# Experts' weights split as pairs of rows, the one-hot table as one VectorE operation, and a buffer of its own for the weighted result

## The chip, the core and the metric

The kernel runs on one core of one Trainium2 chip. The metric is the device time of one execution in microseconds (us); the median of three runs of the kernel before is 1759.38 us. The engines are called PE (TensorE, with PEld for its loads of the stationary operand), DVE (VectorE), ACT (ScalarE), POOL (GpSimd) and SP (SyncE, which here only issues DMA transfers).

## The reference

One layer of a hybrid diffusion model: 1024 latent tokens and 256 context tokens of width 1024 go through differential attention and a gated delta rule, and then the latent tokens through a mixture of 16 experts. Only this last part is touched by the change:

```python
def expert_choice_ffn(h, w_router, w_gate, w_up, w_down):
    def route_set(t):
        n = t.shape[0]
        cap = CAP_FACTOR * n // N_EXPERTS                      # 128 tokens for each expert
        aff = jax.nn.softmax((t @ w_router).astype(jnp.float32), axis=-1)
        gate, idx = lax.top_k(aff.T, cap)                      # each expert chooses its tokens
        xe = t[idx]                                            # 16 x 128 x 1024
        hid = jax.nn.silu(jnp.einsum('ecd,edf->ecf', xe, w_gate)) * jnp.einsum('ecd,edf->ecf', xe, w_up)
        ye = jnp.einsum('ecf,efd->ecd', hid, w_down) * gate[..., None].astype(t.dtype)
        return jnp.zeros_like(t).at[idx.reshape(-1)].add(ye.reshape(-1, t.shape[-1]))
...
x_new = x + gt1 * (jnp.concatenate([o_da, o_gdn], axis=-1) @ w_out)
x_new = x_new + gt2 * expert_choice_ffn(modulate(x_new, norm2_g, sh2, sc2), w_router, w_gate, w_up, w_down)
return rms_norm(x, final_g)
```

Each expert has three float32 matrices of 1024 x 1024 (4 MB each), so that 192 MB of weights are read once, for 128 tokens per expert.

## The kernel before, in words

Products of float32 are made in three passes of a rounded format: each operand is split into a rounded part (`hi`) and its rest (`lo`), and `mm3` (L167) adds hi x hi, lo x hi and hi x lo in PSUM. For one weight row of 1024 values per partition ("a row" below, 128 partitions x 1024) that is 6 matmuls of 128x512, since 1024 columns fill two PSUM banks.

The expert stage (`_experts`) takes, for each expert e, 12 loads of 1 MB, four for each of `w_gate`, `w_up` and `w_down`. `weights` (L1448) issues the load on SP into a buffer `raw` of a ring (`_Ring`; 9 + MORE + 1 buffers in turn) and splits its two rows one after the other: ACT copies the rounded part (`whi`, L1460), DVE subtracts it from the raw row (`wlo`, L1461; for the first few loads POOL does). `whi` and `wlo` have 5 buffers each (WHI, WLO). A raw buffer is free for the next load when its last `wlo` is done; a `whi` or `wlo` buffer is free when PE has used it.

PE's work for an expert is `up` (8 rows of gate into `pgu`, 8 rows of up into `pgv`, in turns of two) and, an expert later, `down` (8 rows of down into `py`): 144 matmuls and 16 transposes. After `up`, ACT takes silu of `pgu` into `hid` (L1505) and DVE multiplies it with `pgv` (L1506); `turned` (L1472) transposes `hid` on PE into the PSUM tile `ptm` and splits it into `hTh` (ACT) and `hTl` (DVE). In the same way the gathered tokens `xe` become `xTh` and `xTl`. `pgu` and `pgv` have one buffer each, so that the next expert's first matmul into `pgu` waits until ACT has read it for `hid`. After `down`, `scatter` weights `py` into `y` on DVE (L1525) and POOL adds its rows to the result in DRAM by an indirect DMA. The tile `y` shares its one buffer with `hid` (tag "hid", YT).

`lists` (L1406) makes an expert's list of tokens two experts ahead: a one-hot table of 128 x 8 x 128, eight `tensor_scalar` operations of 128x128 on DVE for the first four experts and on POOL for the others; eight small matmuls into `pls`, three tiny DVE operations (`ls`, `idx`, `gate`), and then POOL can gather the tokens.

Each engine works through its own queue in order. The order in the queues comes from the scheduler of the tile framework, which places the instructions ahead of time by its own estimates; the kernel's text gives dependencies and priorities only. What stands where is read below from the orders of the two programs.

Of the kernel before, what the change touches and what calls it, by code (L numbers as in the profile page):

```python
"""Hybrid diffusion layer: differential attention and a gated delta rule side by side, then an
expert-choice mixture of experts, on one core.

float32 products of width 256 and more run as three float32r passes over operands that are split
exactly into a rounded part and its rest (h*h + l*h + h*l); narrower ones run in float32.
"""
# [22 lines left out]
P = 128  # L29
# [40 lines left out]
MORE = 6  # L70
WAIT = (16, 17, 18)
YT, RT = "hid", "xe"
WHI, WLO = 5, 5
# [3 lines left out]
# the tokens that the scans finish first come first  # L77
# [31 lines left out]
class _K:  # L109
# [7 lines left out]
    def after(self, dst, src):  # L117
        """A load to dst waits until src is there."""
        self.nc.gpsimd.tensor_copy(dst, src)

    def slot(self, kind, i=None, name=None, dt=F32):
        """A buffer of the queries' or keys' size; in turn, those first that the last head's projections leave first."""
        if i is None:
            order = (0, 1) if kind == "KL" else (0, 2, 1)
            i = order[self.turn[kind] % len(order)]
            self.turn[kind] += 1
        return self.qk.tile([P, L if kind == "QS" else LT], dt, name=name or kind, tag=f"{kind}{i}")
# [4 lines left out]
    def xT(self, kt, t, n):  # L132
        """The two parts of x^T for tiles t to t + n of a group."""
        t0 = max(g for g in self.XT if g <= t)
        return [x[:, kt, (t - t0) * P:(t - t0 + n) * P] for x in self.XT[t0]]
# [9 lines left out]
    def rsqrt_steps(self, pool, x, n, np_=P, tag=""):  # L145
        """1/sqrt(x) for positive x [np_, n]: three Newton steps from the bit estimate."""
# [22 lines left out]
    def mm3(self, out, ah, al, bh, bl, start, stop):  # L169
        """out (+)= a.T @ b in float32, from the split operands."""  # L170
# [10 lines left out]
def _decays(K, pg, ps):  # L181
    """Decays and betas of the delta rule: [token, direction, chunk, head]."""
# [55 lines left out]
def _prep(K, pg, ps, h, kvq):  # L238
    """Norms and decays of a head's chunks, their matrices and the inverses of the 16 x 16 diagonal blocks.

    With k = r k~ (k~ before its l2 norm), c = beta r^2, N = (k~ k~^T) * decay, a chunk of 128 tokens is
        u' = (I + N c)^-1 (v / r - e^G k~ S),   S' = e^Gl S + k~^T (c e^(Gl-G) u'),
        o  = r_q (e^G q~ S + ((q~ k~^T) * decay) c u').
    Both directions share a matrix: below the diagonal the forward one, above it the backward one.
    """
# [29 lines left out]
    # queries with the decay from their chunk's start, one set per direction  # L275
# [59 lines left out]
    # a 16 x 16 block per partition, by substitution  # L335
# [11 lines left out]
    def both(t, fwd, bwd, rows, cols):  # L347
        """A part of both directions' blocks, from an element of each on."""
# [3 lines left out]
    for j in range(15):  # L352
        # forward: rows after j gain their multiple of row j; backward: rows before 15 - j
# [16 lines left out]
def _inproj(K, banks):  # L370
    """Modulation, x^T and the input projection."""
# [7 lines left out]
    with tc.tile_pool(name="p1v", bufs=1, reuse_waits="tile") as pv, \  # L379
# [21 lines left out]
        # v of the attention and a, b of the delta rule, tokens on partitions  # L401
# [15 lines left out]
    # the rest, channels on partitions  # L417
# [109 lines left out]
def _modulation(K, pe, ps, psm):  # L527
    """Shift and scale of both token sets, channels on partitions; loads the first tokens on the way."""
# [23 lines left out]
    # silu(c), silu(c_ctx)  # L552
# [10 lines left out]
    for kt in range(KT):  # L563
# [4 lines left out]
        # of the last tile the scales in float32 at once, the shifts from split parts  # L568
# [26 lines left out]
def _tokens(K, pe, ps, xts, late):  # L595
    """x^T, modulated and split."""
# [31 lines left out]
def _row_vectors(K, pool, ps):  # L628
    """Gate 1, shift 2, scale 2 and gate 2 as rows in DRAM."""
# [29 lines left out]
def _mix(K, prep, left):  # L659
    """Differential attention and the delta rule's scans, side by side."""  # L660
# [3 lines left out]
    with tc.tile_pool(name="g", bufs=1, side="right", reuse_waits="tile") as pg, \  # L664
# [29 lines left out]
        # the first tokens of the output projection, in the buffers that the attention leaves  # L694
# [13 lines left out]
def _mixed(K, t, ol, oh, lo):  # L708
    """The parts of a tile's transposed mix."""
# [12 lines left out]
def _weights(K, pw):  # L722
    """The parts of most of w_out, in the buffers that the last head's scan leaves."""
# [14 lines left out]
    # what the attention's last head leaves  # L738
# [8 lines left out]
    # what is left of them takes the parts of the last head's mix  # L747
# [4 lines left out]
def _weight(K, k, hi, lo, raw):  # L752
    """The parts of a tile of w_out, its columns scaled by the gate."""
# [10 lines left out]
def _delta(K, pg, pw, gps, ps):  # L764
    """Inverses from the 16 x 16 blocks up, T <- T - T (off-diagonal block) T, and the scans of both directions."""
# [27 lines left out]
    def levels(h, st, c0, n):  # L793
        """Doubles the blocks up to the chunk, then W and U of both directions."""
# [50 lines left out]
    def all_levels(h, st):  # L845
        """The chunks' groups in interleaved streams."""
# [4 lines left out]
    # the context's chunks come first  # L851
# [14 lines left out]
    def scan(h, st, step):  # L866
        """One chunk of each direction."""
# [27 lines left out]
    def outputs(st, step):  # L895
        """Both directions' outputs of the last two steps, chunks ascending."""
# [15 lines left out]
    def finish(h, st, inner):  # L912
        """Gated norm of the inner or the outer chunks; they go to the transposed mix."""
# [55 lines left out]
def _head(K, h):  # L969
    """Queries' parts stacked; the keys' rounded parts twice, their rests once: passes of depth 128 and 64."""  # L970
# [19 lines left out]
def _attention(K, pa, ps):  # L990
    """Latent queries over latent and context keys; the two softmax halves of a head in turn."""
# [9 lines left out]
    # the first tiles lie where the projection ends last: these are needed later than queries and keys  # L1001
# [100 lines left out]
def _outproj(K):  # L1102
    """Output projection, gated residual, the router and the experts' inputs; returns what the experts need."""
# [3 lines left out]
    with tc.tile_pool(name="o", bufs=1, side="right", reuse_waits="tile") as po, \  # L1107
# [26 lines left out]
        def setup():  # L1134
            """Rows and columns for the norm, and the router's constants."""
# [3 lines left out]
            # with h = r x (1 + scale) g + shift, h @ w = r (x @ ((1 + scale) g w)) + shift @ w  # L1139
# [18 lines left out]
        def half(j, xn, oh, ol, pp=None, done=0, between=None):  # L1158
            """Adds half of the gated projection to x."""
# [8 lines left out]
        def square(xn, j, h2, ss):  # L1168
            """Half of x's mean square; the guard with the first."""
# [36 lines left out]
        def modulated(t, xn, rs, h2):  # L1206
            """The experts' inputs."""
# [11 lines left out]
        def behind(i):  # L1219
            """The router's part for a tile."""  # L1220
# [3 lines left out]
        for i, t in enumerate(order):  # L1224
# [18 lines left out]
            if not i:  # L1243
                # the last two parts of the weights come late
# [36 lines left out]
class _Ring:  # L1281
    """Buffers of weights, in turn."""
# [15 lines left out]
class _Route:  # L1298
    """Each expert's CAP best tokens (ties: lower index) as slots; an expert's list comes from `lists`."""

    def __init__(self, K, pt, keep, po):
# [10 lines left out]
        # the affinities, and their upper halves: enough against thresholds of twelve bits  # L1312
# [5 lines left out]
    def spread(self, t, ax, bank):  # L1318
        """Eight copies of each expert's affinities, on partitions."""
# [7 lines left out]
    def slots(self, ps):  # L1327
# [9 lines left out]
        # what a slot collects: its token's index in two parts, its weight in three  # L1337
# [10 lines left out]
        # greatest threshold that CAP values reach, three bits a round  # L1348
        th = icst[:, 9:10]
        for it in range(10):  # L1350
# [8 lines left out]
            # the next threshold but for the count's share: in float32 while that has bits enough  # L1359
# [12 lines left out]
        # every token sees its experts' thresholds: above them, and on them  # L1372
# [12 lines left out]
    def places(self, aff, thr, mk, ng, r1, m1, slot):  # L1385
        """Slots of some experts' tokens; -1 without one."""
# [3 lines left out]
        # how many come before a token, and how many are above in all  # L1390
# [7 lines left out]
        # ties enter while there is room: their slots follow the greater ones  # L1398
# [7 lines left out]
    def lists(self, e, ps):  # L1406
        nc, po, slot, val = self.K.nc, self.keep, self.slot, self.val
        iota = self.fcst[:, :P]
        eng = nc.vector if e < 4 else nc.gpsimd
        oh = po.tile([P, NT, P], BF16, name="onehot", bufs=1)  # L1410
        for t in range(NT):
# [254 lines left out]
```

## Time and profile before

| | |
|---|---|
| three runs | 1756.13, 1759.38, 1769.11 us |
| profiled execution | span 1753.3 us (first to last instruction on the core; the profile gives no other time of it) |
| busy in the span | PE 1596.4 (91%), DVE 1315.1 (75%), ACT 916.2 (52%), POOL 609.9 us (35%) |
| chain that ended last | PE 65%, DVE 6%, DMA 5%, POOL 3%, ACT 3%, issue 2% |
| experts' part of the span | about 1132 to 1712 us; the final norm follows |

A timeline row gives start, duration, engine, line, operation, output<-inputs, shape and how many in a row; in brackets the idle time before it and what ended that. When several instructions of a kind run without a gap, the duration covers them all. A single instruction's duration includes an end that the next one overlaps, so the distance from start to start is shorter than the duration.

### The profile page before, as it was taken

How to read it: one execution, taken by the hardware profiler on the slowest of the kernel's cores; microseconds unless marked ns; L12 is line 12 of the kernel's file. 1: busy time of each engine (PE TensorE's matmuls, PEld its weight loads, DVE VectorE, ACT ScalarE, POOL GpSimd, SP SyncE). 2: the span in 40 equal slices, each digit the busy share in tenths (PEclk: the TensorE clock that was granted, in tenths of full speed). 3: DMA queues.
4: the chain of work that ended last, by engine and by line, in shares of the span. 5: the costliest groups of instructions: out<-in, count | busy, mean ns of one | idle time of the engine just before them, and what ended most of it. 6: DMA issues, size and time to landing. Idle time of an engine off the chain costs nothing.

```text
span 1753.3 us, 24640 instructions
## 1 busy us (share of the span) xinstructions
PE 1596.4 (91%) x8793; PEld 1303.7 (74%) x8793; DVE 1315.1 (75%) x2110; ACT 916.2 (52%) x1514; POOL 609.9 (35%) x489
## 2 busy tenths in 40 slices
PE   6999899899979999999999998399999999999990
PEld 2897678788857878787787787278888877777780
DVE  6657845678667776667777744789999989989894
ACT  6521125434324545455465232287777777777773
POOL 3013321332244662371630122434565334441012
PEclk9999899999989999999999999599999999999995
DMA  7478852443564042412212484799999999999915
GB/s 268 154 250 249 246 169 92 155 128 118 162 183 114 24 103 91 109 48 74 85 54 100 143 307 167 265 359 358 399 385 398 399 384 353 357 360 375 369 37 216
DMA packets 170846, 377.17 MB, mean 215 GB/s; under 512 B 32542, under 2 KB 82140, under 8 KB 169572
## 3 DMA queue, kind: packets, MB, share of 16 engines
q1 hardware_dynamic: 131874, 315.22, 49.5%
q0 software_dynamic: 11664, 43.52, 8.3%
q10 hardware_dynamic: 27186, 16.86, 3.8%
q8 instruction: 69, 1.13, 0.3%
q14 instruction: 53, 0.43, 0.1%
HBM read 315.60 MB, written 55.76 MB: 212 GB/s over the span
## 4 chain that ended last, share of the span: by engine, by line
PE 65%; DVE 6%; DMA 5%; POOL 3%; ACT 3%; issue 2%; SPq 0%; ACTq 0%; POOLq 0%; DVEq 0%
PE sp L1028 4%; PE pgu L172 3%; PE po L1055 3%; PE sp L1027 3%; PE pgu L173 3%; PE pgu L174 3%; PE pgv L172 3%; PE pgv L174 3%; PE pgv L173 3%; PE py L173 3%; PE py L172 3%; PE py L174 3%; PE ptr L1049 2%; PE pp L172 2%; PE pp L173 2%
## 5 line engine op out<-in xcount | busy, mean ns | idle before, releaser
L1461 DVE TENSOR_TENSOR wlo<-raw,whi 128x1024 fp32r<-128x1024 f32 x376 | 453.3, 1241 | 40.8 <-ACT whi L1460 31.6
L1460 ACT ACTIVATE whi<-raw 128x1024 fp32r<-128x1024 f32 x384 | 399.1, 1059 | 134.0 <-PE pgu L173 53.5
L1412 POOL TENSOR_SCALAR onehot<-fcst,slot 128x128 bf16<-128x128 f32 x96 | 156.9, 2027 | 42.9 <-PE pls L1415 22.5
L173 PE MATMUL pl<-XH,wl 128*128 128x512 f32 x384 | 152.9, 398 | 3.7 <-DVE wl L178 3.7
L172 PE MATMUL pl<-XH,wh 128*128 128x512 f32 x384 | 153.2, 399 | 0.9 <-DVE ab L413 0.9
L174 PE MATMUL pl<-XL,wh 128*128 128x512 f32 x384 | 153.1, 399 | 0.0
L1030 DVE TENSOR_REDUCE mx<-sp 128x1 f32<-128x1280 f32 x64 | 95.2, 1487 | 54.5 <-PE sp L1028 54.1
L1526 POOL DMA_INDIRECT acc_dram<-y,idx x15 | 36.1, 2409 | 279.6 <-DVE y L1525 265.6
L172 PE MATMUL pgu<-whi,xTh 128*128 128x512 f32 x256 | 102.1, 399 | 18.1 <-ACT hid L1505 18.1
L1033 ACT ACTIVATE pt<-sp,mx 128x1280 f32<-128x1280 f32 x64 | 84.8, 1325 | 57.4 <-DVE mx L1030 54.1
L174 PE MATMUL pgu<-wlo,xTh 128*128 128x512 f32 x256 | 101.8, 398 | 0.0
L172 PE MATMUL pgv<-whi,xTh 128*128 128x512 f32 x256 | 101.7, 397 | 0.0
L173 PE MATMUL pgu<-whi,xTl 128*128 128x512 f32 x256 | 100.8, 394 | 0.0
L174 PE MATMUL pgv<-wlo,xTh 128*128 128x512 f32 x256 | 100.4, 392 | 0.0
L1027 PE MATMUL sp<-KH,QS 128*128 128x512 f32 (+1 forms) x192 | 89.3, 465 | 12.0 <-ACT pt L1033 6.8
L173 PE MATMUL pgv<-whi,xTl 128*128 128x512 f32 x256 | 99.7, 390 | 0.0
L174 PE MATMUL py<-wlo,hTh 128*128 128x512 f32 x240 | 94.6, 394 | 0.7 <-POOL wlo L1461 0.7
L172 PE MATMUL py<-whi,hTh 128*128 128x512 f32 x240 | 93.8, 391 | 0.0
L173 PE MATMUL py<-whi,hTl 128*128 128x512 f32 x240 | 93.6, 390 | 0.0
L1028 PE MATMUL sp<-KL,QS 64*128 64x512 f32 (+1 forms) x192 | 89.6, 467 | 0.0
L1055 PE MATMUL po<-V,aT 128*128 128x128 f32 x640 | 88.7, 277 | 0.0
L172 PEld LDWEIGHTS pl<-XH,wh 128*128 128x128 f32 x384 | 73.2, 191 | 20.3 <-issue 5.2
(540 smaller groups left out, 4008.1 us busy)
## 6 DMA issues: line engine op xcount, KB each, us to landing
raw<-w_gate SPq DMA_DIRECT2D x64, 1024.0 KB
raw<-w_up SPq DMA_DIRECT2D x64, 1024.0 KB
raw<-w_down SPq DMA_DIRECT2D x64, 1024.0 KB
rwm<-w_mod POOLq DMA_DIRECT2D x32, 512.0 KB, 6.3
wr<-w_in ACTq DMA_DIRECT2D x24, 512.0 KB
wm<-w_mod SPq DMA_DIRECT2D x8, 1024.0 KB
KH<-qk_dram SPq DMA_DIRECT2D x16, 320.0 KB
xt<-x SPq DMA_DIRECT2D x8, 512.0 KB
```

Source lines behind the costliest of these rows:

```text
L172: nc.tensor.matmul(out, ah, bh, start=start, stop=False)
L173: nc.tensor.matmul(out, al, bh, start=False, stop=False)
L174: nc.tensor.matmul(out, ah, bl, start=False, stop=stop)
L1027: nc.tensor.matmul(sp[:, k0:k1], qs, st["KH"][s][:, k0:k1], start=True, stop=False)
L1028: nc.tensor.matmul(sp[:, k0:k1], qs[64 * s:64 * s + 64], st["KL"][64 * s:64 * s + 64, k0:k1], start=False, stop=True)
L1030: nc.vector.tensor_reduce(mx, sp[:, :LT], axis=AX.X, op=ALU.max, negate=True)
L1033: nc.scalar.activation(pt, sp[:, :LT], AF.Exp, bias=mx, accum_out=sm)
L1055: nc.tensor.matmul(po, aT[c], st["V"][:, c], start=c == 0, stop=c == NTT - 1)
L1412: eng.tensor_scalar(oh[:, t], iota, slot[:, t, e:e + 1], None, op0=ALU.is_equal)
L1460: nc.scalar.activation(hi, raw[:, i], AF.Copy)
L1461: eng.tensor_tensor(lo, raw[:, i], hi.bitcast(F32), ALU.subtract)
L1526: nc.gpsimd.indirect_dma_start(out=K.acc_dram, in_=y, in_offset=None, compute_op=ALU.add, out_offset=bass.IndirectOffsetOnAxis(ap=ready[e] ...
```

## The change

- `weights` loads a pair of rows per partition as one piece of 8 KB (partition p gets rows 2p and 2p + 1 of a block of 256) instead of rows p and p + 128 as two pieces of 4 KB, and splits both rows with one ACT operation and one subtraction of 128x2048.
- `whi` and `wlo` have 3 buffers of two rows each in place of 5 of one row.
- `turned` takes every second column of the tokens (or of `hid`) so that the transposed operand fits the new row order: the transposes read with a step of 2.
- `lists` makes the one-hot table for all experts by one DVE `tensor_tensor` of 128x1024 with both inputs broadcast.
- `y` has a buffer of its own. The ring of raw buffers has 14 in place of 16.

```diff
-MORE = 6
+MORE = 4
-YT, RT = "hid", "xe"
-WHI, WLO = 5, 5
+RT = "xe"
+WHI, WLO = 3, 3
@@ lists
-        eng = nc.vector if e < 4 else nc.gpsimd
         oh = po.tile([P, NT, P], BF16, name="onehot", bufs=1)
-        for t in range(NT):
-            eng.tensor_scalar(oh[:, t], iota, slot[:, t, e:e + 1], None, op0=ALU.is_equal)
+        nc.vector.tensor_tensor(oh, _bc_t(iota, NT), _bc_f(slot[:, :, e], NT), ALU.is_equal)
@@ weights
-            nc.sync.dma_start(raw, w[0, e].rearrange("(k p) f -> p k f", p=P)[:, 2 * j:2 * j + 2])
+            nc.sync.dma_start(raw, w[0, e].rearrange("(j p i) f -> p j i f", p=P, i=2)[:, j])
             eng = nc.gpsimd if e == 0 and (j == 0 or w is a["w_gate"] and j == 1) else nc.vector
-            his, los = [], []
-            for i in range(2):
-                hi = pm.tile([P, FF], F32R, name="whi", bufs=WHI)
-                lo = pm.tile([P, FF], F32R, name="wlo", bufs=WLO)
-                nc.scalar.activation(hi, raw[:, i], AF.Copy)
-                eng.tensor_tensor(lo, raw[:, i], hi.bitcast(F32), ALU.subtract)
-                his.append(hi)
-                los.append(lo)
-            return his, los
+            hi = pm.tile([P, 2, FF], F32R, name="whi", bufs=WHI)
+            lo = pm.tile([P, 2, FF], F32R, name="wlo", bufs=WLO)
+            K.split(hi, lo, raw, eng)
+            return [hi[:, i] for i in range(2)], [lo[:, i] for i in range(2)]
@@ turned
-                c = (4 * j + i) * P
-                nc.tensor.transpose(p[:, i], src[:, c:c + P], ident)
+                c = (2 * j + i // 2) * 2 * P
+                nc.tensor.transpose(p[:, i], src[:, c + i % 2:c + 2 * P:2], ident)
@@ scatter (and the same for the last expert)
-            y = pm.tile([P, D], F32, name="y", tag=YT)
+            y = pm.tile([P, D], F32, name="y")
```

`K.split` (L176) is the ACT copy into `hi` and the subtraction into `lo`. With the buffers and the lengths the scheduler's order changes too. On ACT, the queue around the `hid` of a late expert reads before (`whi` x8 ahead of `hid` are the eight rows of the expert-before's `down`):

```order
L1460 ACTIVATE whi<-raw 128x1024 x3
L177 ACTIVATE xTh_13756<-ptm 128x512
L1460 ACTIVATE whi<-raw 128x1024 x8
L1505 ACTIVATE hid<-pgu 128x512 x2
L1460 ACTIVATE whi<-raw 128x1024 x3
L177 ACTIVATE hTh_13815<-ptm 128x512
L177 ACTIVATE hTh_13868<-ptm 128x512
```

and now, around the `hid` of one of the later experts:

```order
L177 ACTIVATE whi<-raw 128x2048 x2
L177 ACTIVATE hTh_12660<-ptm 128x512
L177 ACTIVATE whi<-raw 128x2048 x2
L177 ACTIVATE hTh_12705<-ptm 128x512
L177 ACTIVATE whi<-raw 128x2048 x4
L177 ACTIVATE xTh_12808<-ptm 128x512
L177 ACTIVATE whi<-raw 128x2048 x3
L1499 ACTIVATE hid<-pgu 128x512 x2
L177 ACTIVATE whi<-raw 128x2048
L177 ACTIVATE xTh_12889<-ptm 128x512
```

Before, `hid` of a late expert stood behind all eight rows of `down`; now at most two of the four pairs of `down` are copied ahead of it in any expert. For the experts 10 and 13 none is: `hid` stands directly behind `up`'s last pair and `down`'s first comes after it.

On DVE, the queue around the `hid` of a late expert (9 or 10) and the list of a later one now reads as follows; before it had neither a one-hot table nor anything longer than a row:

```order
L178 TENSOR_TENSOR wlo<-raw,whi 128x2048
L1500 TENSOR_TENSOR hid<-pgv,hid 128x512 x2
L178 TENSOR_TENSOR wlo<-raw,whi 128x2048
L178 TENSOR_TENSOR xTl_13170<-ptm,xTh_13169 128x512
L178 TENSOR_TENSOR wlo<-raw,whi 128x2048 x3
L178 TENSOR_TENSOR hTl_13221<-ptm,hTh_13220 128x512
L178 TENSOR_TENSOR wlo<-raw,whi 128x2048 x2
L178 TENSOR_TENSOR hTl_13266<-ptm,hTh_13265 128x512
L1415 COPY ls<-pls 128x5
L1410 TENSOR_TENSOR onehot<-fcst,slot 128x1024
L178 TENSOR_TENSOR wlo<-raw,whi 128x2048
```

Two pairs of `down` stand ahead of `hid` for the experts up to 7 and the last one; for the experts 8 to 14 one pair or none does. The half `hTl`, `ls` and the table stand together between two splits.

## Rows read from the trace of the kernel before

**Rows 1.** Busy time by window: window, its length, PE, PEld, DVE, ACT, POOL, clock, DMA, GB/s

```profile
1340.00:1370.00 30.00, 30.00 (x137) 24.83 (x137) 28.77 (x30) 24.32 (x26) 14.60 (x8) 1.00 1.03 394
1600.00:1640.00 40.00, 37.84 (x182) 30.99 (x181) 36.17 (x39) 30.07 (x33) 5.86 (x3) 1.00 0.97 356
5.00:10.00 5.00, 0.42 (x1) 0.18 (x1) 1.96 (x6) 2.29 (x5) 0.54 (x1) 1.00 1.01 412
```

**Rows 2.** PE's timeline at two places of one period

```profile
1399.64 0.39 PE L172 MATMUL py<-whi,hTh 128*128 128x512 f32 x1
...
1402.13 0.39 PE L174 MATMUL py<-wlo,hTh 128*128 128x512 f32 x1
...
1408.90 1.03 PE L1478 MATMUL ptm<-ident,hid 128*128 128x128 f32 x8
1409.69 0.48 PE L172 MATMUL pgv<-whi,xTh 128*128 128x512 f32 x1
```

**Rows 3.** DVE's timeline: first lists, one early boundary, four starts of y

```profile
1125.70 1.70 DVE L1412 TENSOR_SCALAR onehot<-fcst,slot 128x128 bf16<-128x128 f32 x8
...
1252.86 1.29 DVE L1506 TENSOR_TENSOR hid<-pgv,hid 128x512 f32<-128x512 f32 x2 [0.68 <-ACT whi L1460]
...
1256.93 4.62 DVE L1461 TENSOR_TENSOR wlo<-raw,whi 128x1024 fp32r<-128x1024 f32 x4
...
1264.65 1.28 DVE L1525 SCALAR_TENSOR_TENSOR y<-py,gate,gt 128x1024 f32<-128x1024 f32 x1 [0.23 <-PE py L174]
...
1299.51 1.28 DVE L1525 SCALAR_TENSOR_TENSOR y<-py,gate,gt 128x1024 f32<-128x1024 f32 x1 [0.23 <-PE py L174]
...
1635.07 1.28 DVE L1525 SCALAR_TENSOR_TENSOR y<-py,gate,gt 128x1024 f32<-128x1024 f32 x1
...
1671.98 1.28 DVE L1525 SCALAR_TENSOR_TENSOR y<-py,gate,gt 128x1024 f32<-128x1024 f32 x1
```

**Rows 4.** PE's waits, 1090 to 1753 us: total us, times, longest

```profile
PE pgu L172 <- ACT hid L1505: 18.1, 9, 2.2
...
PE py L174 <- POOL wlo L1461: 0.7, 1, 0.7
```

**Rows 5.** The chain that ended last at one boundary: start, us, what

```profile
1439.79 1.04 ACT whi L1460
1440.83 0.98 ACT hid L1505 x2
...
1441.85 0.50 PE pgu L172
```

**Rows 6.** SP's waits, 1090 to 1753 us

```profile
SPq L1454 <- DVE wlo L1461: 420.7, 164, 5.1
```

**Rows 7.** ACT's timeline at the same boundary

```profile
1438.83 2.00 ACT L1460 ACTIVATE whi<-raw 128x1024 fp32r<-128x1024 f32 x2 [0.98 <-PE py L173]
1440.74 1.06 ACT L1505 ACTIVATE hid<-pgu 128x512 f32<-128x512 f32 x2
```

**Rows 8.** Groups by line, 1090 to 1753 us: total busy, mean ns, idle before

```profile
L1461 DVE TENSOR_TENSOR wlo<-raw,whi 128x1024 fp32r<-128x1024 f32 x376 | 453.3, 1241 | 40.8 <-ACT whi L1460 31.6 <-PE pgv L174 1.6
L1460 ACT ACTIVATE whi<-raw 128x1024 fp32r<-128x1024 f32 x384 | 399.1, 1059 | 134.0 <-PE pgu L173 53.5 <-PE pgv L173 36.2 <-PE py L173 35.6
L1412 POOL TENSOR_SCALAR onehot<-fcst,slot 128x128 bf16<-128x128 f32 x96 | 156.9, 2027 | 42.9 <-PE pls L1415 22.5 <-DVE wlo L1461 20.3
...
L178 DVE TENSOR_TENSOR xTl<-ptm,xTh 128x512 fp32r<-128x512 f32 x34 | 22.9, 681 | 4.7 <-ACT xTh L177 4.7
...
L1478 PEld LDWEIGHTS ptm<-ident,xe 128*128 128x128 f32 x128 | 16.1, 145 | 8.4 <-issue 5.3
...
L1412 DVE TENSOR_SCALAR onehot<-fcst,slot 128x128 bf16<-128x128 f32 x32 | 6.9, 285 | 0.0
```

**Rows 9.** Groups by line and shape, whole span: splits of 896

```profile
L177 ACT ACTIVATE oh<-raw 128x896 fp32r<-128x896 f32 x5 | 4.8, 951 | 13.1 <-DMA raw<-ot_dram 6.8 <-PE pp L174 6.4
...
L178 DVE TENSOR_TENSOR lo<-raw,oh 128x896 fp32r<-128x896 f32 x5 | 5.4, 1086 | 1.6 <-ACT oh L177 1.5
```

More of the change, by code (lines that the diff above doesn't have):

```diff
@@ L1579, in _experts @@
         with tc.high_priority():
-            y = pm.tile([P, D], F32, name="y", tag=YT)
+            y = pm.tile([P, D], F32, name="y")
             nc.vector.scalar_tensor_tensor(y, py, ready[last][1], gt2, op0=ALU.mult, op1=ALU.mult)
```

## The prediction

> **What bounds the kernel now.** I read the busy time by window first: in the experts' stage PE is busy for 30.00 of 30 us at 1340 us and 37.84 of 40 at 1600 us, at a granted clock of 1.00 [rows 1]. That is the 2.4 GHz level, so the clock has nothing to give. DVE stands close behind with 28.77 of 30 and 36.17 of 40, and ACT has a fifth to spare. The reader is to see a stage whose length is PE's work plus what PE waits. PE's timeline gives the work: from 1399.64 to 1402.13 us eleven matmuls start, so one costs 0.226 us, and eight transposes take 0.79 us from 1408.90 to 1409.69 [rows 2]. A row of weights is six matmuls, 1.36 us, and a pair of rows 2.72 us.
>
> DVE's timeline gives the period, from one `y` to the next: 34.86 us early (1264.65 to 1299.51) and 36.91 us late (1635.07 to 1671.98) [rows 3]. PE's waits explain the difference of 2.05 us: `pgu <- ACT hid`, 18.1 us in 9 times, 2.2 us at most [rows 4]. The chain of waits shows how it arises: a copy `whi` ends, then `hid` runs for 0.98 us, then PE starts `pgu` [rows 5]. On ACT's timeline that copy had to wait 0.98 us for PE to free a `whi` buffer, and `hid` stood behind it [rows 7]. So `hid`, whose input was long ready, was held by copies queued ahead of it. The loads are not the bound: SP waits 420.7 us for ring buffers that `wlo` frees [rows 6], and no wait of PE on a weight load is among its waits.
>
> **The change, part by part.**
>
> *The position of `hid`, removed stall.* By the order of the changed program at most two pairs of `down` stand ahead of `hid` instead of eight rows, so nothing ahead of it waits for PE to get through `down`. The 18.1 us [rows 4] go. Late next is the split of `down`'s first pairs, below.
>
> *DVE's load for an expert.* A subtraction of 512 columns takes 681 ns and one of 896 takes 1086 [rows 8, 9], 1.055 ns per column, so 2048 columns take 1086 + 1152 x 1.055 = 2.30 us. In a row some 0.09 overlaps (1024 columns would be 1.22 each, and four take 4.62 [rows 3]), which leaves 2.21 from start to start. The upper bound is twice the mean of a row, 2 x 1.241 = 2.48 [rows 8], as if nothing fixed were saved. On ACT 896 columns take 951 ns and 1024 take 1059 [rows 8, 9], so a pair takes 1059 + 8 x 108 = 1.92 us. Twelve pairs are 26.5 us on DVE, `hid` 1.2, `y` 1.2 [rows 3], four halves of `xTl` and `hTl` at 0.6 (0.681 less the overlap [rows 8]) 2.4, the list's small operations 0.3. New is the one-hot table: nearest are a 1024-wide subtraction of two tensors at 1.16 to 1.24 us [rows 3, 8] and the eight `tensor_scalar` that DVE made for the first experts, 1.70 us [rows 3]; I take 1.15, since it is one instruction of 1024 columns, and keep 1.70 for the range. The sum is 32.6 to 32.7 of a period of 34.86 us: no overload, 2.2 us spare. The table leaves POOL, whose eight operations took 2.0 us each [rows 8]; POOL was never awaited for them by PE, so that gives nothing. For the first four experts DVE saves 0.5 us each, off the path.
>
> The Trainium skill ("VectorE: DVE Perf Modes", "The perf-mode tier table") speaks against this edit: in float32 `tensor_scalar` runs at twice the rate of `tensor_tensor`, 1227 against 2293 ns for 2048 elements. By it the table would cost an estimated 1.15 us where eight `tensor_scalar` cost 0.6. The 1.70 us of the trace disagrees for pieces of 128 columns, and the sum goes by the trace.
>
> *The slack of a split.* PE needs a row 5 or a pair 3 buffers after the one that frees its buffer, so in both programs 5.44 us pass between the release and the need (four rows of 1.36, two pairs of 2.72). Before, copy and subtraction took 1.06 + 1.24 and some 0.2 of hand-over: 2.9 us of slack. Now they take 1.92 + 2.30 + 0.2: 1.0 us. `lo` is only needed by the third matmul, 0.45 us later, in both. Whatever stands between two splits on ACT or DVE for longer than that now reaches PE. This is the price of the change, and I work it out where the order shows such a place.
>
> - Boundaries with one pair of `down` ahead of `hid` on DVE (experts 8, 9, 11, 12, 14): if `up` ends at T, `hid` starts at T + 0.45 (a matmul's 0.39 [rows 2] and a hand-over), takes 1.2, and the second pair's split 2.30, done at T + 3.95. PE needs it at T + 2.72 + 0.45 = 3.17. That is 0.8 us, five times: 4.0.
> - Boundaries with none ahead (10 and 13): `pgu` ends at T - 2.3, `hid` on ACT 1.06, `xTh` 0.6, the first pair's copy 1.92 to T + 1.2, its subtraction to T + 3.5, needed at T + 0.45. About 3.0 us, twice: 6.0.
> - The bunch `hTl`, `ls`, table, `hTl` (experts 9 to 12) puts up to 2.4 us between splits against 1.0 + 0.45 of slack and what 0.5 us per pair (2.72 less 2.21) has gained; 0.5 each, 2.0.
> - The last three boundaries start with transposes of `xe` whose halves `xTh`, `xTl` (0.6 + 0.68 [rows 8]) PE then waits for: about 0.9 each, 2.7.
>
> Together 14.7 us come back, with bounds of 9 (the slack accrued covers bunches and half of the rest) and 18.
>
> *Edits taken at nothing.* Ring of 14 instead of 16: an expert's 12 loads in 34.86 us are one in 2.9 us, so the lead is still 14 x 2.9 = 40 us; at 394 to 412 GB/s [rows 1] 1 MB takes 2.5 to 2.7 us, so a load keeps up even where no lead is left. Pieces of 8 KB instead of 4: the modulation's loads, already rows of 2048 floats, moved at 412 GB/s [rows 1], as fast as the experts' loads; nothing either way. `y`'s own buffer: it frees the order of `hid`, counted above. POOL's first split of `down` becomes one of 4.7 us where PE waited 0.7 [rows 4]: -0.7 to +1.6, taken as 0.
>
> *Transposes with a step of 2.* 256 of them; 0.79 / 8 = 0.099 us each [rows 2], their load of the operand 0.145 [rows 8]. The trace has no such load with a step, so its bounds are 0 and a doubled pitch, 256 x 0.099 = 25 us. I take 0: PE's neighbouring loads hide beside matmuls, and a piece of 128 columns has the same number of elements.
>
> The Trainium skill ("Advanced Engine Details and Errata", "Memory Cachelines") has SBUF lines of 16 bytes and full rate from two hits on a line; a step of 2 in float32 still hits each line twice. By it the term is 0; no row here shows it.
>
> **Sum.** -18.1 + 14.7 = -3.4 us on a span of 1753.3: 1749.9. The median of the runs, 1759.4, lies 6.1 above the span, so I predict a median of **1756 us**, with 1750 to 1762 by the bounds of the returned stall.
>
> **The rivals.** A measurement of this kernel can tell 1% (17.6 us) from no change, about; faster is below 1741.8, slower above 1777.
>
> 1. *All stalls go and none comes back* (0.14): the halves ready early absorb the long splits, and every period is 34.86 us. 1759.4 - 18.1 = 1741. For it speaks that DVE's load fits on average; against it that the slack of a split falls from 2.9 to 1.0 us at places whose order is bad. Half of this case lies beyond 1%.
> 2. *The other side: the strided operand reads at half rate* (0.07). 256 transposes cost 0.099 us more: 1756 + 25 = 1781. It decides from a pitch of about 0.18 us per transpose. Nothing in the trace speaks for or against.
> 3. *DVE becomes the bound* (0.12). With pairs at 2 x 1.241 = 2.48 (no saving), the table at 1.70 and the rest 5.1 an expert takes 36.6 us on DVE, above 34.86. Fifteen periods lose 1.7 each, 26 in all, less 18.1: 1767. It decides from a split of 2.34. Against it: the fixed part of a split is paid once per pair now.
> 4. *The change doesn't move the stall* (0.07): PE still waits at the boundary, now for `hid` behind copies of pairs, and the 14.7 us are added: 1774. Against it is the order of ACT's queue.
>
> The forecast itself has 0.60.
>
> **Range and chances.** 1743 to 1771 leaves out half of the first rival, the second, and parts of the third and fourth: about 0.19. Faster by over 1%: half of rival 1 and a little of the forecast, 0.11. Slower: rival 2 and the tails of 3 and 4, 0.12. Within 1%: 0.77.
>
> **What would show it.** In the changed kernel's PE waits `pgu <- ACT hid` should be nearly gone, and waits of `py` and `pgu` on `wlo`, `whi` and `xTl` of 9 to 18 us stand in its place, at the boundaries of experts 8 to 15. A pair's split should take about 2.30 us on DVE and 1.92 on ACT, the table about 1.2, eight transposes 0.79 from their start to the next matmul, and DVE should be busy for some 93% of the stage. I would be wrong if early periods, where the trace before shows no stall, become longer than 34.9 us, if weight loads appear among PE's waits, or if the transposes' pitch changes.

## The result and the profile after

The changed kernel is slower by half a per cent: a median of 1770.68 us against 1762.44 us (20 runs each), ratio 1.0052 with a 95% interval of 1.0039 to 1.0064. I had forecast 1756 us, a gain of 3.4; the time lies just inside the range, but on the other side of the old one. The profiled execution has a span of 1768.9 us (its run took 1770.7). That of before had 1753.3, which the 20 runs show to be one of its lowest.

So the two spans must be cut into parts before they are compared. The marks are rows of the timelines: VectorE's last `ax<-oex` (all tokens are through the router), its copy `tb<-th` (the thresholds are found), TensorE's first `pgu`, its last `py`, the end. Each row is taken by its start. Before:

```profile
1092.22 1.96 DVE L1203 TENSOR_SCALAR ax<-oex,osm 128x128 f32<-128x128 f32 x1
...
1119.67 0.23 DVE L1373 COPY tb<-th 128x128 f32<-128x128 f32 x1
...
1131.98 0.79 PE L172 MATMUL pgu<-whi,xTh 128*128 128x512 f32 x1
...
1711.93 0.39 PE L174 MATMUL py<-wlo,xTh 128*128 128x512 f32 x1
```

After:

```profile
1096.68 1.96 DVE L1203 TENSOR_SCALAR ax<-oex,osm 128x128 f32<-128x128 f32 x1
...
1129.87 0.23 DVE L1373 COPY tb<-th 128x128 f32<-128x128 f32 x1
...
1141.49 0.79 PE L172 MATMUL pgu<-whi,xTh 128*128 128x512 f32 x1
...
1721.17 0.39 PE L174 MATMUL py<-wlo,xTh 128*128 128x512 f32 x1
```

| part, us | before | after | difference |
|---|---|---|---|
| up to the last `ax` | 1092.2 | 1096.7 | +4.5 |
| search of the thresholds | 27.45 | 33.19 | +5.74 |
| first lists and gather | 12.31 | 11.62 | -0.69 |
| experts' stage (`pgu` to `py`) | 579.95 | 579.68 | -0.27 |
| tail | 41.37 | 47.73 | +6.36 |

The first part is the same program in both. In the twelve runs below that mark lies between 1091.7 and 1101.3 us, whatever the kernel, so I take its 4.5 us as chance. The other parts make +11.1 us, against 8.2 in the medians (6.9 to 11.3 by the interval).

**The stage** has the forecast durations on VectorE and ScalarE, but it ends only 0.27 us shorter. TensorE's waits of the kernel after (total us, times, longest) answer to [rows 4]:

```profile
PE py L174 <- DVE wlo L178: 4.8, 5, 1.6
PE ptm L1472 <- DMA xe<-h_dram,idx: 5.2, 1, 5.2
PE ptm L1472 <- DVE xTl L178: 1.7, 1, 1.7
PE pgu L172 <- ACT xTh L177: 1.5, 2, 1.3
PE pgu L172 <- ACT hid L1499: 1.5, 1, 1.5
PE pgu L174 <- DVE wlo L178: 1.4, 2, 1.1
```

The wait on `hid` fell from 18.1 to 1.5 us. Waits on `wlo`, `xTl` and `xTh` took its place (the `xe` line is the first gather and was there before). With the small ones the stage idles 11.8 us instead of 18.8. The groups by line (busy us, mean ns) show the sizes, and answer to [rows 8]:

```profile
L178 DVE TENSOR_TENSOR wlo<-raw,whi 128x2048 fp32r<-128x2048 f32 x188 | 427.0, 2292 | 45.5 <-ACT whi L177 44.4
L177 ACT ACTIVATE whi<-raw 128x2048 fp32r<-128x2048 f32 x192 | 367.2, 1918 | 131.1 <-PE py L173 43.2 <-PE pgu L173 42.7 <-PE pgv L173 41.1
L1472 PEld LDWEIGHTS ptm<-ident,hid 128*128 128x128 f32 x128 | 19.9, 203 | 5.0 <-DVE xTl L178 2.7
L1410 DVE TENSOR_TENSOR onehot<-fcst,slot 128x1024 bf16<-128x1024 f32 x16 | 19.5, 1216 | 0.0
L1472 PEld LDWEIGHTS ptm<-ident,xe 128*128 128x128 f32 x128 | 18.4, 206 | 6.5 <-issue 5.2
```

A pair's split takes 2.292 us (forecast 2.30) and its copy 1.918 (1.92), the table 1.216. But the load of the transposes' operand went from 145 to 206 ns (`xe`; [rows 8] have it before). Two rows of TensorE's timeline show what is left of that on the path:

```profile
1249.21 1.11 PE L1472 MATMUL ptm<-ident,xe 128*128 128x128 f32 x8
1250.07 0.47 PE L172 MATMUL pgu<-whi,xTh 128*128 128x512 f32 x1
```

Eight transposes now take 0.86 us where [rows 2] had 0.79. Cut by what TensorE does, the stage has 7.0 us less of waits, 3.4 us more of transposes (26.7 against 23.3) and 3.4 us more of matmuls.

**The search** is where the first large loss lies. VectorE's timeline, and GpSimd's at the same time:

```profile
1103.29 1.28 DVE L1354 TENSOR_SCALAR_CACHE_REDUCE raw<-raw,th 128x1024 bf16<-128x1024 bf16 x1
...
1104.50 3.81 DVE L1364 TENSOR_TENSOR base<-th,icst 128x1 f32<-128x1 int32 x1
1108.82 1.28 DVE L1354 TENSOR_SCALAR_CACHE_REDUCE raw<-raw,th 128x1024 bf16<-128x1024 bf16 x1
...
1110.03 2.73 DVE L1364 TENSOR_TENSOR base<-th,icst 128x1 f32<-128x1 int32 x1
```

```profile
1103.79 13.40 POOL L178 TENSOR_TENSOR wlo<-raw,whi 128x2048 fp32r<-128x2048 f32 x3
```

The reader is to see one element per partition taking 3.81 us, and three pair-long subtractions of GpSimd running under it. In the kernel before the same two operations, beside row-long subtractions, read:

```profile
1100.03 1.65 DVE L1364 TENSOR_TENSOR base<-th,icst 128x1 f32<-128x1 int32 x1
1103.40 0.58 DVE L1364 TENSOR_TENSOR base<-th,icst 128x1 f32<-128x1 int32 x1
```

The six of them cost 9.7 us instead of 4.1, in a serial chain of operations, each of which needs the one before.

**The tail** is the second. TensorE's last matmul for expert 14 and VectorE's queue after it:

```profile
1710.52 0.39 PE L174 MATMUL py<-wlo,hTh 128*128 128x512 f32 x1
```

```profile
1709.72 2.29 DVE L178 TENSOR_TENSOR wlo<-raw,whi 128x2048 fp32r<-128x2048 f32 x1 [0.24 <-ACT whi L177]
1712.67 2.29 DVE L178 TENSOR_TENSOR wlo<-raw,whi 128x2048 fp32r<-128x2048 f32 x1 [0.65 <-ACT whi L177]
1714.88 1.28 DVE L1519 SCALAR_TENSOR_TENSOR y<-py,gate,gt 128x1024 f32<-128x1024 f32 x1
```

`py` was ready at 1710.91, and `y` started 3.97 us later, behind two splits of the last expert. The final norm reads the rows that this `y` is scattered to, so the end moves with it. In the kernel before `y` started 0.04 us after its `py`:

```profile
1701.28 0.39 PE L174 MATMUL py<-wlo,hTh 128*128 128x512 f32 x1
```

```profile
1701.71 1.28 DVE L1525 SCALAR_TENSOR_TENSOR y<-py,gate,gt 128x1024 f32<-128x1024 f32 x1 [0.38 <-PE py L174]
```

From there the 6.36 us can be followed to the end: 3.93 are `y`'s later start, 1.20 the scatter, which landed 8.06 us after its issue instead of 6.86, and the rest, 1.2, comes after the landing.

### The profile page after: what moved, and what is told of

The parts are those of the page before. It is cut to its first block, busy times and chain, and to the rows that moved or that the text cites. A ratio compares the mean times of both kernels' runs of the same rounds, so it can differ in the third digit from the quotient of the medians.

```text
span 1768.9 us, 23761 instructions
## 1 busy us (share of the span) xinstructions
PE 1603.6 (91%) x8793; PEld 1308.6 (74%) x8793; DVE 1304.4 (74%) x1906; ACT 884.6 (50%) x1322; POOL 485.1 (27%) x389
## 4 chain that ended last, share of the span: by engine, by line
PE 63%; DVE 8%; DMA 5%; issue 4%; POOL 3%; ACT 3%; SPq 0%; POOLq 0%; ACTq 0%; DVEq 0%
PE sp L1028 4%; PE po L1055 3%; PE sp L1027 3%; PE pgu L174 3%; PE pgu L173 3%; PE pgu L172 3%; PE py L174 3%; PE pgv L174 3%; PE pgv L173 3%; PE pgv L172 3%; PE py L172 3%; PE py L173 3%; DMA qe<-eg_dram 2%; PE ptr L1049 2%; PE pp L172 2%
## 5 line engine op out<-in xcount | busy, mean ns | idle before, releaser
L178 DVE TENSOR_TENSOR wlo<-raw,whi 128x2048 fp32r<-128x2048 f32 x188 | 427.0, 2292 | 45.5 <-ACT whi L177 44.4
L177 ACT ACTIVATE whi<-raw 128x2048 fp32r<-128x2048 f32 x192 | 367.2, 1918 | 131.1 <-PE py L173 43.2
L1520 POOL DMA_INDIRECT acc_dram<-y,idx x15 | 63.5, 4233 | 365.9 <-DVE y L1519 365.9
L173 PEld LDWEIGHTS pl<-XH,wl 128*128 128x128 f32 x384 | 73.8, 192 | 20.5 <-DVE wl L178 4.2
```

What stands on the lines that cost most here:

```text
L173: nc.tensor.matmul(out, al, bh, start=False, stop=False)
L177: self.nc.scalar.activation(hi, src, AF.Copy)
L178: (eng or self.nc.vector).tensor_tensor(lo, src, hi.bitcast(F32), ALU.subtract)
L1520: nc.gpsimd.indirect_dma_start(out=K.acc_dram, in_=y, in_offset=None, compute_op=ALU.add, out_offset=bass.IndirectOffsetOnAxis(ap=ready[e] ...
```

## The experiments

Theory A: three costs eat the gain. GpSimd's pair-long subtractions hold the search; the step of 2 lengthens the transposes; the last-but-one `y` stands behind pair-long splits. Its rival B: the longer splits only move the stall within the stage, and search and tail are chance. In what follows the ratios are to the kernel before, and the parts come from the same marks as above. The traces speak against chance at once: the search takes 27.5 us in the three runs that leave the kernel before's search and splits as they were (before, b1_yown, b2_onehot1) and 33.2 in the five with the changed kernel's (after, x2_lastrows, x3_rows4k, x5_y14, u1_yhid); the tail takes 41.4 to 42.3 us in the first three, and 47.0 to 47.7 in after, x3_rows4k and x4_search, which end alike.

**GpSimd's subtractions by rows** (x1_poolrows).

```diff
-            K.split(hi, lo, raw, eng)
+            if eng is nc.gpsimd:
+                nc.scalar.activation(hi, raw, AF.Copy)
+                for i in range(2):
+                    eng.tensor_tensor(lo[:, i], raw[:, i], hi[:, i].bitcast(F32), ALU.subtract)
+            else:
+                K.split(hi, lo, raw, eng)
```

> The changed kernel, but GpSimd's first subtractions (the three pairs of the first expert that it splits while VectorE searches the router's thresholds) are made row by row, 128x1024, in place of 128x2048. Theory A (VectorE's small two-tensor operation L1364 waits until GpSimd's running subtraction ends, so a longer one holds each of the serial rounds longer): the six L1364 take about 4 us in all as in the kernel before (1.65 + 5 x 0.6) instead of 9.7, the search is some 5 us shorter, and the ratio to the kernel before falls from 1.0052 to about 1.002. Rival (the difference of the search is chance or comes from the loads beside it): L1364 stays at 9 to 10 us and the ratio at 1.005.

```profile
L1364 DVE TENSOR_TENSOR base<-th,icst 128x1 f32<-128x1 int32 x6 | 4.6, 760 | 0.0
```

The search fell to 27.84 us, as A said, but the ratio stayed at 1.0049 (1.0030 to 1.0069). The scheduler had ordered the stage anew, and it became 6.9 us longer (5.4 us of waits of `py` on `y` are new). The forecast of the search held, that of the ratio missed; the next test keeps the order.

**The search's operation without a second tensor** (x4_search).

```diff
+        icf = po.tile([P, 7], F32, name="icf")
+        nc.vector.tensor_copy(icf, icst[:, 0:7])
...
-                nc.vector.tensor_tensor(base, th, icst[:, it:it + 1], ALU.add)
+                nc.vector.tensor_scalar(base, th, icf[:, it:it + 1], None, op0=ALU.add)
```

> The changed kernel with one operation of the router's search written otherwise: L1364 adds a per-partition scalar (a float copy of the constants, made once) instead of adding two tensors; the orders of the engines are the same otherwise. Theory A (an operation with two SBUF inputs waits for GpSimd's running subtraction, a one-tensor operation does not): the six L1364 take 0.2 us each instead of 9.7 us in all, the search falls from 33.2 to about 24.5 us, stage and tail stay, ratio 1.0052 - 0.0049 = about 1.000. Rival (the operation is slow beside any GpSimd work, or the search waits for something else): the search stays over 30 us, ratio 1.004 to 1.005.

```profile
L1366 DVE TENSOR_SCALAR base<-th,icf 128x1 f32<-128x1 int32 x6 | 1.3, 209 | 0.0
```

The same sums beside the same subtractions of GpSimd take 1.3 us. The search is 25.51 us, 7.7 less, the tail 47.72 as in the changed kernel, and the ratio 1.0004 (0.9989 to 1.0020). Both tests together show the first large cost: with two tensor inputs the operation waits for the GpSimd subtraction beside it, and longer when that subtraction is longer. The Trainium skill ("SBUF — State Buffer", "Who interferes with whom") says that a VectorE instruction with two SBUF inputs contends with a GpSimd instruction that reads SBUF, and that the ports which the two share are locked by one of them at a time; the 3.81 against 0.21 us agree.

**Old row layout** (x3_rows4k): two 4 KB pieces per load, transposes without a step, the orders unchanged.

```diff
-            nc.sync.dma_start(raw, w[0, e].rearrange("(j p i) f -> p j i f", p=P, i=2)[:, j])
+            nc.sync.dma_start(raw, w[0, e].rearrange("(k p) f -> p k f", p=P)[:, 2 * j:2 * j + 2])
...
-                nc.tensor.transpose(p[:, i], src[:, c + i % 2:c + 2 * P:2], ident)
+                nc.tensor.transpose(p[:, i], src[:, c:c + P], ident)
```

> The changed kernel with the old row layout: two pieces of 4 KB per load and transposes that read neighbouring columns; the orders of all engines stay the same. Theory A (the step of 2 lengthens TensorE's load of the transposes' operand, part of which shows): the loads fall from 0.205 to about 0.143 us, eight transposes from 0.87 to 0.79 us, the stage by 2.6 us, ratio about 1.0037; nothing in the loads changes. Rival (pieces of 8 KB are what costs or helps): the transposes' times stay, and waits on ring buffers or weight loads move instead; ratio off by more than 3 us either way.

```profile
L1472 PEld LDWEIGHTS ptm<-ident,hid 128*128 128x128 f32 x128 | 15.7, 140 | 6.5 <-DVE xTl L178 2.7
L1472 PEld LDWEIGHTS ptm<-ident,xe 128*128 128x128 f32 x128 | 15.6, 145 | 7.5 <-issue 5.4
```

The loads are back at 140 and 145 ns, and the transposes' time on the path fell from 26.7 to 24.5 us and the stage by 2.57. The ratio, 1.0049 (1.0030 to 1.0067), can't tell 2.6 us from none; the trace can. The Trainium skill ("Advanced Engine Details and Errata", "Memory Cachelines"), by which the step would cost nothing, does not hold for this operand: 206 against 145 ns.

**`y` back in `hid`'s buffer** (u1_yhid), the change otherwise.

```diff
-            y = pm.tile([P, D], F32, name="y")
+            y = pm.tile([P, D], F32, name="y", tag="hid")
```

> The changed kernel with y back in hid's buffer. Theory A (y's own buffer is what freed hid from behind the copies on ScalarE): hid stands behind all four pairs of down again from expert 5 on, PE's wait pgu on hid comes back with 20 to 30 us (ten or eleven boundaries at 2 to 3 us), ratio 1.015 to 1.02. Rival (the pairs with 3 buffers freed it): the wait stays under 5 us and the ratio at 1.005.

```profile
PE pgu L172 <- ACT hid L1499: 23.4, 9, 2.7
```

Ratio 1.0187 (1.0164 to 1.0210): the stall is back and the stage 17 us longer. It was `y`'s own buffer, not the pairs, that freed `hid`.

**`y`'s own buffer alone**, in the kernel before (b1_yown); one raw buffer makes room for it.

```diff
-MORE = 6
+MORE = 5
...
-            y = pm.tile([P, D], F32, name="y", tag=YT)
+            y = pm.tile([P, D], F32, name="y", tag="y")
```

> The kernel before with a buffer of its own for y and nothing else (the ring has 15 buffers instead of 16 to make room). Theory A: the wait of pgu on hid (18.1 us) goes, and with rows of 1024 the slack of a split is 2.9 us, so that at most 3 to 5 us come back; search and transposes as before; ratio 0.991 to 0.994. Rival B (whatever removes the hid stall moves it to waits on wlo and to the last y, as in the changed kernel): waits of 10 us or more appear, ratio 0.998 to 1.002.

```profile
PE py L172 <- DVE y L1525: 4.6, 2, 3.9
PE ptm L1478 <- DVE xTl L178: 3.2, 4, 0.8
PE pgu L172 <- ACT xTh L177: 2.6, 4, 0.8
PE py L174 <- DVE wlo L1461: 2.0, 5, 0.7
PE pgu L172 <- ACT hid L1505: 0.8, 1, 0.8
```

Ratio 0.9994 (0.9980 to 1.0007): A missed, its rival was right for the stage. The `hid` stall is gone and the new order of the queues makes four other waits, although the splits are short. So the returned waits are a matter of the order, not only of the pair's length.

**The one-hot table alone**, in the kernel before (b2_onehot1).

```diff
-        for t in range(NT):
-            eng.tensor_scalar(oh[:, t], iota, slot[:, t, e:e + 1], None, op0=ALU.is_equal)
+        nc.vector.tensor_tensor(oh, _bc_t(iota, NT), _bc_f(slot[:, :, e], NT), ALU.is_equal)
```

> The kernel before with the one-hot table as one VectorE operation and nothing else. Theory A (the table costs VectorE 1.2 us in an expert and is hidden; GpSimd's work was off the path): stage, search and tail within 2 us of before, the hid stall stays at about 18 us, ratio 0.998 to 1.001. Rival (the table's 1.2 us on VectorE reach TensorE): waits on wlo of 5 us or more, ratio 1.003 or more.

Ratio 0.9990 (0.9975 to 1.0006), the `hid` stall 18.3 us, stage, search and tail within 0.8 us of before. The table is hidden, as forecast.

**The last expert's splits by rows** (x2_lastrows).

```diff
+            if e == NE - 1 and w is a["w_down"]:
+                for i in range(2):
+                    K.split(hi[:, i], lo[:, i], raw[:, i], eng)
+            else:
+                K.split(hi, lo, raw, eng)
```

> The changed kernel with the last expert's down pairs split row by row on ScalarE and VectorE. Theory A (the weighted result of expert 14 starts 3.96 us after its last matmul because two pair-long subtractions stand ahead of it on VectorE, and everything to the end hangs on its scatter): it starts at most 1.5 us late, the tail from TensorE's last matmul to the end falls from 47.7 to 44.5 to 45.5 us, ratio about 1.0035. Rival (the tail is longer for the scatter's or the loads' own time): the tail stays over 47 us.

A miss: ratio 1.0051 (1.0032 to 1.0070), tail 47.10 us, `y` 4.77 us late. The scheduler put five rows ahead of `y` instead of two pairs. What counts is the place, so the next run moved that.

**`y` of expert 14 ahead of the last expert's third split** (x5_y14); `ys` holds the `y` tiles.

```diff
+            if e == NE - 1 and w is a["w_down"] and j == 2:
+                nc.vector.tensor_copy(lo[:, 0, 0:1], ys[-1][:, 0:1])
             K.split(hi, lo, raw, eng)
```

> The changed kernel with one tiny VectorE copy that makes the split of the last expert's third down pair wait for the weighted result y of expert 14, so that y goes ahead of it in the queue. Theory A (the tail hangs on y of expert 14, which stands behind two pair-long subtractions): y starts at most 1.2 us after its last matmul instead of 3.96, the stage's end may slip by up to 3.4 us, but the time from the last matmul of expert 14 to the end falls by 2.8 us or more, ratio 1.0052 - 0.0016 to 1.0030. Rival (the end hangs on the last expert's matmuls): what y gains the later split loses, ratio 1.005 or more.

```profile
1712.53 0.39 PE L174 MATMUL py<-wlo,hTh 128*128 128x512 f32 x1
```

```profile
1711.73 2.29 DVE L178 TENSOR_TENSOR wlo<-raw,whi 128x2048 fp32r<-128x2048 f32 x1 [0.24 <-ACT whi L177]
1713.94 1.28 DVE L1522 SCALAR_TENSOR_TENSOR y<-py,gate,gt 128x1024 f32<-128x1024 f32 x1
1715.25 0.15 DVE L1458 CAST wlo<-y 128x1 fp32r<-128x1 f32 x1
1717.17 4.49 DVE L178 TENSOR_TENSOR wlo<-raw,whi 128x2048 fp32r<-128x2048 f32 x2 [1.76 <-ACT whi L177]
```

`y` starts 1.02 us after its `py`; TensorE then waits longer (the stage is 3.35 us longer), and still the ratio is 1.0011 (0.9994 to 1.0029), 0.4% below the changed kernel's. From expert 14's last matmul to the end it is 50.6 us instead of 58.0. Of these 7.4 us 2.95 are `y`'s start. 1.8 are the scatter, which landed 6.27 us after its issue instead of 8.06: its issue on GpSimd took 1.55 us, with VectorE idle between the copy and the next split, instead of 3.35 with a pair-long split beside it (rows of the changed kernel, then of this run; more in the last section):

```profile
1716.43 3.35 POOL L1520 DMA_INDIRECT acc_dram<-y,idx  x1 [16.90 <-DVE y L1519]
```

```profile
1715.49 1.55 POOL L1523 DMA_INDIRECT acc_dram<-y,idx  x1 [13.96 <-DVE wlo L1458]
```

The rest, 2.7 us, comes after the landing; the order of the norm's steps differs there, which I did not test apart.

**Versions.** Four further kernels leave out waits that were found; `FPOOL = ()` takes GpSimd's multiplications out of the final norm, where VectorE's small operations waited 2.2 us for each.

```diff
-FPOOL = (1,)
+FPOOL = ()
```

v1_best_after is the changed kernel with this, the old row layout and x4_search's operation:

> A version: the changed kernel with the old row layout (no step in the transposes), the one-tensor L1364, and the final norm without GpSimd (FPOOL empty: VectorE scales all its rows). Theory A: search 33.2 to 24.5, transposes -2.3, and a tail without VectorE's small operations waiting 2.2 us for GpSimd's multiplication four times, some 4 us shorter: 15 us less than the changed kernel, ratio 0.996 to 0.998. Rival (such waits are hidden behind the DMAs of the tail): ratio 0.999 to 1.001.

Ratio 0.9975 (0.9959 to 0.9992): search 25.51, tail 42.33 us, 5.4 less. v2_best_before is the kernel before with the new operation and `FPOOL = ()`:

> A version: the kernel before with the one-tensor L1364 and the final norm without GpSimd. Theory A: the six L1364 take 1 us instead of 4.1, so the search is 3 us shorter, the tail 4 us shorter, the stage with its hid stall as before: ratio 0.996. Rival (hidden): 0.999 to 1.001.

0.9965 (0.9949 to 0.9982); search 24.53, tail 36.68. v6_before adds the one-hot table:

> A version: v2_best_before with the one-hot table as one VectorE operation. Theory A: GpSimd has nothing to do beside the splits, one wait on it (0.7 us) goes, ratio 0.995 to 0.9965. Rival: VectorE's 1.2 us per expert show, ratio 0.998 or more.

0.9932 (0.9908 to 0.9955), less than the 0.995 expected at best; its profiled run is the slowest of six and does not show why. v4_after is v1_best_after with x5_y14's copy and one buffer moved:

```diff
-MORE = 4
+MORE = 3
-WHI, WLO = 3, 3
+WHI, WLO = 4, 3
```

> A version: v1_best_after with y of expert 14 moved ahead as in x5_y14, and four buffers for whi paid for with one raw buffer (MORE 3, WHI 4). Theory A: 2.8 us less in the tail, and one more pair of slack on ScalarE's side takes off some waits, 0 to 3 us: ratio 0.994 to 0.996. Rival (the other order moves waits elsewhere): 0.997 to 1.000.

Ratio **0.9912** (0.9886 to 0.9938), a median of 1745.35 us (6 runs): it is faster than both kernels. I had expected 0.994 to 0.996; what the extra buffer gives was not tested apart. Its search takes 25.50 us, the stage 572.79, the tail 37.68, with `y` 0.04 us after its `py`; what is left of TensorE's waits in the stage:

```profile
PE pgu L174 <- DVE wlo L178: 3.1, 3, 1.1
PE py L174 <- DVE wlo L178: 3.0, 3, 1.6
PE pgv L174 <- DVE wlo L178: 2.2, 4, 1.2
PE pgu L172 <- ACT hid L1503: 1.3, 1, 1.3
```

## Why the prediction was wrong

- **The removed stall, right:** 18.1 us forecast, 16.6 gone, and u1_yhid shows that `y`'s buffer did it.
- **The returned waits, right in kind, too large:** 14.7 us forecast, 9.9 measured. The durations of a pair's split and copy were right to 1%, and no wait on weight loads appeared, so the ring of 14 and the 8 KB pieces cost nothing that shows. But the waits are a matter of the order too: b1_yown has 12.5 us of waits with short splits, 4.6 of them on `y`.
- **The transposes, mis-sized:** taken as 0, with a bound of 25 us; x3_rows4k gives 2.2 us on the path, where the whole rise is 3.4. Two of the signs that I had named for being wrong came with it: the transposes' pitch moved, and an early period, from one `y` (1276.16) to the next (1311.19), became 35.03 us instead of 34.86.
- **The matmuls, not in the sum:** they take 537.9 us instead of 534.6. Both traces have a short stretch at half clock in the stage (a granted clock of 0.50 at 1623 to 1626 us after, at 1554 to 1557 before; more below); what else lengthens them was not tested.
- **The step that failed:** "POOL's first split of `down` becomes one of 4.7 us ... taken as 0". I costed GpSimd's longer subtractions only where TensorE waits for their result, at one place. The three others run while VectorE makes the serial search, and I never asked what VectorE does beside them. The rows were there: in the trace before, L1364 takes 1.65 and 0.58 us for one element. x4_search gives 7.7 us back by that operation alone; the change had lengthened the search by 5.74, and this operation in it by 5.6.
- **The other missing term:** the tail was taken as unchanged. I worked out at what boundaries the order puts pair-long splits ahead of something urgent, but only for TensorE; the last-but-one `y`, on which scatter and final norm hang, stands behind two of them. x5_y14 moves its start from 3.97 to 1.02 us and the ratio from 1.0052 to 1.0011; 2.95 us of that are the start itself and 1.8 the scatter's issue, and the cause of the rest stays open.

With the stage at -0.3 instead of -3.4, the search at +5.7 and the tail at +6.4 the sum has the other sign. Of the rivals none named a place outside the stage, so it is luck that the time lies inside the range. Two sums of the forecast are also wrong, and neither decides: VectorE's terms for an expert add to 32.75 us, not 32.6 to 32.7, and the bounds of 9 and 18 us for the returned stall give a median of 1750 to 1759, not 1762.

## What to carry to other kernels

An operation that becomes longer must be priced against every engine that shares something with it while it runs, not only against whoever waits for its result: look in the trace for tiny operations with long durations beside it. Before an edit reorders queues, follow the last link of the chain that ends the program (here `y`, scatter, norm) through the new order as closely as the busy stage. And a stall that comes from a queue's order need not go without leaving another: of the 18.1 us here 16.6 went, 9.9 came back as other waits, and transposes and matmuls took the rest.

## What the runs showed of the hardware

A wait can cost TensorE more than its length. In u1_yhid, after a wait of 2.75 us, matmuls start 0.43 us apart instead of 0.227 for some microseconds; by window (columns as in [rows 1]) the granted clock is 1.00 (2.4 GHz) before, and 0.50 (1.2 GHz) after it:

```profile
1640.00:1650.00 10.00, 9.31 (x42) 7.37 (x40) 9.03 (x5) 7.29 (x6) 0.00 (x0) 1.00 1.00 400
1653.00:1658.00 5.00, 5.00 (x13) 3.90 (x12) 1.55 (x3) 0.84 (x1) 0.00 (x0) 0.50 0.98 372
```

Not every wait does this: eight of that run's waits on `hid` last 2.75 us, and after three of them the granted clock stays at 1.00. In that run 23.4 us of waits on `hid` came with about 9 us more for matmuls than in the kernel before (543.4 against 534.6).

And a VectorE split lengthens the scatter's issue on GpSimd, which took 4.23 us on average in the changed kernel against 2.41 before. In u1_yhid seven of the fifteen issues start while no split runs and take 1.57 to 1.59 us; the other eight start under a pair-long split and take 3.35 to 3.69. In v4_after two issues start under seven splits in a row and take 16.66 us; they end 1.5 us after the last of these (the rows of u1_yhid, then of v4_after with its splits):

```profile
1702.63 1.57 POOL L1520 DMA_INDIRECT acc_dram<-y,idx  x1 [38.04 <-DVE y L1519]
```

```profile
1520.96 16.66 POOL L1525 DMA_INDIRECT acc_dram<-y,idx  x1 [20.35 <-DVE gate L1420]
```

```profile
1520.66 15.49 DVE L178 TENSOR_TENSOR wlo<-raw,whi 128x2048 fp32r<-128x2048 f32 x7
```

These are readings of kept traces; apart from x5_y14, where the copy holds the next split back, no run changed the split under an issue.
